# Seven products of quarters in place of eight in the second product of a feed forward, and low halves of weights made by adding transfers

## The chip, the cores and the metric

One core of a Trainium2 chip runs the whole program. The metric is its device time in microseconds (us), taken over several executions of the same compiled kernel. TensorE (PE) multiplies matrices, VectorE (DVE), ScalarE (ACT) and GpSimd (POOL) work element by element, and SyncE (SP) mainly issues transfers (DMA) between the large memory (HBM) and the on-chip memory (SBUF). Results of PE land in PSUM.

## The reference

Two layers of a decoder on one sequence of 512 tokens with 1024 channels, in float32. A layer mixes the tokens in three ways (pooling means, a state-space layer called S5, sparse attention), merges these, and then applies a squared-ReLU feed forward of width 4096. Cut to the part in question, with `x` 512 x 1024:

```python
def feed_forward_part(x):            # once in each of two layers
    h = jnp.square(jax.nn.relu(x @ w_ff1))        # 512 x 4096
    return layer_norm(ALPHA * x + h @ w_ff2, ln2_g, ln2_b)
```

The second product is `h @ w_ff2`, 512 x 4096 by 4096 x 1024. The next layer's S5 needs operands that depend on its parameters alone.

## The kernel before, in words

**One float32 product as three.** Every operand is split into a high half `hi` (the value rounded to the type that PE multiplies in one pass) and a low half `lo = value - hi`. `mm3_` (L91) issues three matmuls for each pair of blocks: hi by hi (L98), hi by lo and lo by hi (L99, L100). A matmul here is of 128 x 128 by 128 x 512.

**A weight.** `wload` (L69) loads 128 x 1024 weights (512 KB) by a transfer of SP into `wst` (two buffers), ACT casts it to `wh` (L82), and DVE, or in some stages POOL, subtracts to get `wl` (L85). `wh` and `wl` have four buffers each in the pool `wp`.

**The feed forward** (`ffn`, L1093, and `feed_forward`, L1224) runs in eight chunks c of 512 hidden channels. `up(c)` makes the chunk's hidden activations in four tiles m: 24 matmuls into PSUM `mm`, relu on ACT (L1102), square on DVE (L1103), split by ACT (L61) and DVE (L62). `down(c)` multiplies them by the chunk's four tiles of `w_ff2`: for each half of the output channels and each block `tb` of 128 tokens, `part` issues 12 matmuls into PSUM `s` or `t`, and DVE adds the result to `xm` (L1120). These are eight groups of 12, 96 matmuls, for a chunk's down, and 96 for its up. The program order is up(c+1), then down(c).

**What goes on beside it.** At the start of a feed forward POOL applies the affine part of the norm before it (`ln_affine`, L217: L222 and L223, 16 operations). In layer 0, `s5_ahead` (L533) then lets POOL build layer 1's S5 operands in four blocks r beside chunks 1 to 6: each loads `bc` (L501, SP), computes into one of two tiles `zwe` (L461 to L464, L514, L524 and others), and stores 1664 KB to `s5d` by SP. Weights `w0` for layer 1's first product are loaded during chunk 2; the weights of chunk 7 as its down begins.

**What sets the order.** A scheduler that simulates the engines' times fixes the order of the instructions of each engine when the program is built; loads of weights have high priority. An engine then runs its list strictly in that order, and each instruction waits for the semaphores that it names.

Of the kernel before, what the change touches and what calls it, by code (L numbers as in the profile page):

```python
# [18 lines left out]
DEPTH = 2  # L19
# [7 lines left out]
class Kern:  # L27
# [463 lines left out]
    def s5_operands(self, pool, i, r, zwe, eng, alone=False):  # L491
# [43 lines left out]
    def s5_ahead(self, i, after):  # L535

        with self.tc.tile_pool(name=f"s5a{i}", bufs=1, reuse_waits="tile") as pool:
            qs = [self.t(pool, [128, 3328], F32, f"zwe{k}") for k in range(2)]
            for r in range(5):
                with self.tc.issue_after(after):  # L540
                    if r < 2:
                        self.nc.gpsimd.memset(qs[r][:, 0:2304], 0.0)
                    if r < 4:
                        self.s5_operands(pool, i, r, qs[r % 2], self.nc.gpsimd, True)
# [548 lines left out]
    def ffn(self, i, xs, p0):  # L1093

        nc, v = self.nc, self.nc.vector

        def up(c):
            hs = []
            for m in range(4):
                ps = p0[m] if c == 0 else self.xw([self.wload(self.A["wf1"][i, 4 * c + m])])[0]  # L1100
                h = self.t(self.mt, [128, 512], F32, "mt")
                nc.scalar.activation(h, ps, AF.Relu)  # L1102
                v.tensor_tensor(h, h, h, OP.mult)  # L1103
                hh, hl = self.pair("ab"[c % 2])
                self.hi_lo(hh, hl, h)
                hs.append((hh, hl))
            return hs
# [22 lines left out]
        def down(c, hs, post):  # L1130
            W = self.A["wf2"]
            if c < 7:
                for half in range(2):
                    ws = [None] * 4
                    for kp in range(2):
                        ws[2 * half + kp] = self.wload(W[i, c, half, kp])
                    for tb in range(4):
                        part(hs, ws, tb, half, c)
# [84 lines left out]

    def feed_forward(self, i, xs, p0, w0p, g, b):  # L1224
        nc, A = self.nc, self.A
        up, down = self.ffn(i, xs, p0)
        how = ("aa", "aa", "am", "vv")

        def post(tb):
# [11 lines left out]
        for c in range(8):  # L1241
            nx = up(c + 1) if c < 7 else None
            if c == 1 and i < DEPTH - 1:
                ahead = self.s5_ahead(i + 1, self.affine.ins)
            if 1 <= c < 7 and i < DEPTH - 1:
                next(ahead, None)
            if c == 2 and i < DEPTH - 1:
                w0 = [self.wload(A["win"][i + 1, j], w0p, nc.vector) for j in range(4)]
            if c == 7 and i < DEPTH - 1:
                g, b = [], []  # L1250
                for q, tag, row in ((g, "hi_a", 4 + 4 * i), (b, "lo_a", 5 + 4 * i)):
# [107 lines left out]
```

## Time and profile before

| | us |
|---|---|
| median of 3 runs | 1770.89 |
| lowest and highest | 1769.59, 1772.9 |
| profiled execution | 1768.97 |
| its span, from first to last instruction | 1767.2 |
| PE busy in the span | 1672.5 (95%) |
| DVE, ACT, POOL busy | 1135.8 (64%), 711.8 (40%), 546.2 (31%) |

The profile shows one execution. Busy shares are means over stages with different limits, so a stage is read from windows and timelines of that stage. In a timeline a row gives start, duration, engine, line and operation, with out<-in, and in brackets the idle time before it with what ended it. The granted clock of PE is given as a share of 2.4 GHz: 1.00 is 2.4 GHz, 0.50 is 1.2 GHz.

### The profile page before, as it was taken

The numbers are of one execution on the slowest core, as the hardware profiler recorded it, in microseconds if no ns is written. First come the engines' busy times: TensorE is split into PE (matmuls) and PEld (weight loads), VectorE is DVE, ScalarE is ACT, GpSimd is POOL, SyncE is SP. The second block draws the span as 40 slices with busy tenths as digits, with TensorE's granted clock in tenths as the row PEclk, the third lists the DMA queues.
The fourth block names the chain that finished last, engine by engine and source line by source line (L and its number), as shares of the span: only waits on it lengthen the run. The fifth ranks groups of instructions, "written<-read, shape, count | busy, mean of one in ns | idle before, by whom it ended". The sixth has DMA issues, their size and how long they took to land.

```text
span 1767.2 us, 22544 instructions
## 1 busy us (share of the span) xinstructions
PE 1672.5 (95%) x8356; PEld 1397.7 (79%) x8356; DVE 1135.8 (64%) x2171; ACT 711.8 (40%) x1245; POOL 546.2 (31%) x636
## 2 busy tenths in 40 slices
PE   3969999999999999999998999999999999999996
PEld 2857887887779888888897788878787888888885
DVE  8797568676578656444576565867657774444447
ACT  2444336666534323233242442555564433222221
POOL 4993421322113999400033233122202050000002
PEclk9989999999999999999998999999999999999998
DMA  5313251111251246443316424211124133333331
GB/s 193 117 37 98 87 184 60 57 51 60 87 188 36 93 143 190 138 139 97 113 61 205 164 88 150 87 60 60 56 88 161 43 119 96 96 97 100 101 97 59
DMA packets 64334, 183.69 MB, mean 104 GB/s; under 512 B 12256, under 2 KB 21216, under 8 KB 63200
## 3 DMA queue, kind: packets, MB, share of 16 engines
q1 hardware_dynamic: 61632, 176.88, 30.9%
q10 hardware_dynamic: 2592, 5.38, 1.0%
q8 instruction: 65, 1.06, 0.3%
q14 instruction: 45, 0.37, 0.1%
HBM read 164.93 MB, written 17.30 MB: 103 GB/s over the span
## 4 chain that ended last, share of the span: by engine, by line
PE 78%; DVE 12%; POOL 4%; DMA 3%; ACT 2%; issue 1%; SPq 0%; DVEq 0%; ACTq 0%; POOLq 0%
PE mm L98 16%; PE mm L99 16%; PE mm L100 16%; PE s L99 4%; PE s L100 4%; PE s L98 4%; PE t L99 3%; PE t L100 3%; PE t L98 3%; PE o L834 3%; PE t L929 2%; DVE wl L85 1%; PE s L901 1%; PE s L900 1%; PE o L801 1%
## 5 line engine op out<-in xcount | busy, mean ns | idle before, releaser
L82 ACT CAST wh<-wst 128x1024 fp32r<-128x1024 f32 (+1 forms) x260 | 270.4, 1042 | 545.7 <-PE s L100 210.9
L85 DVE TENSOR_TENSOR wl<-wst,wh 128x1024 fp32r<-128x1024 f32 (+2 forms) x212 | 281.0, 1327 | 253.0 <-ACT wh L82 252.6
L98 PE MATMUL mm<-xh,wh 128*128 128x512 f32 (+1 forms) x1088 | 429.8, 395 | 6.6 <-ACT wh L82 5.4
L100 PE MATMUL mm<-xh,wl 128*128 128x512 f32 (+1 forms) x1088 | 420.2, 386 | 7.5 <-DVE wl L85 7.5
L99 PE MATMUL mm<-xl,wh 128*128 128x512 f32 (+1 forms) x1088 | 419.1, 385 | 0.0
L100 PEld LDWEIGHTS mm<-xh,wl 128*128 128x128 f32 x1088 | 205.5, 189 | 50.1 <-DVE wl L85 8.8
L98 PEld LDWEIGHTS mm<-xh,wh 128*128 128x128 f32 x1088 | 205.8, 189 | 44.9 <-ACT wh L82 5.9
L99 PEld LDWEIGHTS mm<-xl,wh 128*128 128x128 f32 x1088 | 206.0, 189 | 33.8
L85 POOL TENSOR_TENSOR wl<-wst,wh 128x1024 fp32r<-128x1024 f32 x48 | 122.2, 2546 | 239.2 <-ACT wh L82 233.5
L193 POOL TENSOR_TENSOR xm<-xm,ln_g 128x512 f32<-128x512 f32 x9 | 12.2, 1367 | 321.2 <-ACT xm L192 321.2
L906 ACT ACTIVATE P<-P,mx 128x512 f32<-128x512 f32 (+3 forms) x128 | 71.3, 559 | 63.5 <-DVE mx L904 63.0
L904 DVE CUSTOM_DVE_ANT_0 P<-s,mask 128x512 f32<-128x512 f32 (+3 forms) x128 | 59.6, 484 | 45.3 <-PE s L901 38.1
L62 DVE TENSOR_TENSOR Pl<-t,Ph 128x384 fp32r<-128x384 f32 (+1 forms) x96 | 57.3, 597 | 35.8 <-ACT Ph L61 35.5
L1120 DVE TENSOR_TENSOR xm<-xm,t 128x512 f32<-128x512 f32 x56 | 38.4, 686 | 54.1 <-PE t L100 51.2
L222 POOL TENSOR_TENSOR xm<-xm,hi_a 128x512 f32<-128x512 f32 x8 | 12.7, 1585 | 180.5 <-PE t L238 180.5
L222 POOL TENSOR_TENSOR xm<-xm,ln_g 128x512 f32<-128x512 f32 x16 | 30.2, 1886 | 121.6 <-PE t L238 121.6
L1120 DVE TENSOR_TENSOR xm<-xm,s 128x512 f32<-128x512 f32 x56 | 38.2, 682 | 41.6 <-PE s L100 41.6
L913 POOL TENSOR_SCALAR P<-P,sm,gate 128x128 f32<-128x128 f32 x32 | 15.3, 479 | 156.2 <-DVE sm L908 156.2
L61 ACT CAST Ph<-t 128x384 fp32r<-128x384 f32 (+1 forms) x96 | 48.1, 505 | 26.2 <-PE t L929 26.1
L98 PE MATMUL mm<-hi_a,wh 128*128 128x512 f32 x132 | 54.7, 414 | 2.1 <-DVE lo_a L318 2.1
L1103 DVE TENSOR_TENSOR mt<-mt 128x512 f32<-128x512 f32 x64 | 55.6, 869 | 0.0
L929 PE MATMUL t<-ident,P 128*128 128x128 f32 x320 | 51.8, 276 | 2.7 <-DVE P L913 2.7
(406 smaller groups left out, 3834.3 us busy)
## 6 DMA issues: line engine op xcount, KB each, us to landing
wst<-in_wf_dram SPq DMA_DIRECT2D x128, 512.0 KB, 3.5
wst<-in_win_dram SPq DMA_DIRECT2D x80, 512.0 KB, 3.3
wst<-in_wup_dram SPq DMA_DIRECT2D x24, 512.0 KB, 3.5
wst<-in_wout_dram SPq DMA_DIRECT2D x16, 512.0 KB, 4.2
s5d<-zwe SPq DMA_DIRECT2D x4, 1664.0 KB, 9.2
zwe<-s5d SPq DMA_DIRECT2D x4, 1664.0 KB, 9.1
xd<-xm SPq DMA_DIRECT2D x8, 512.0 KB, 4.9
w<-in_w_dram SPq DMA_DIRECT2D x8, 512.0 KB, 7.6
```

Source lines behind the costliest of these rows:

```text
L62: b = self.nc.vector.tensor_tensor(lo, src, hi.bitcast(F32), OP.subtract)
L82: self.nc.scalar.copy(wh, st)
L85: e.tensor_tensor(wl, st, wh.bitcast(F32), OP.subtract)
L98: mm(out, ah, bh, start=first and i == 0, stop=False, **kw)
L99: mm(out, ah, bl, start=False, stop=False, **kw)
L100: mm(out, al, bh, start=False, stop=last and i == n - 1, **kw)
L834: mm = lambda o, a, b, **k: nc.tensor.matmul(o, a, b, skip_group_check=True, **k)
L904: v.tensor_tensor_reduce(out=p, in0=ss[qb], in1=self.mask[:, 384 - 128 * qb:512], scale=-1.0, scalar=3e38, op0=OP.add, op1=OP.min, accum_o ...
L906: nc.scalar.activation(p, p, AF.Exp, bias=mx[:, qb:qb + 1], scale=-1.0, accum_out=c)
L929: nc.tensor.transpose(pt[:, n:n + 128], P[:, c:c + 128], self.ident)
L1103: v.tensor_tensor(h, h, h, OP.mult)
L1120: v.tensor_tensor(r, r, ps, OP.add)
```

## The change

Chunks 0 to 6 of the second product go by the Strassen-Winograd scheme. The product of a chunk (512 tokens x 512 hidden by 512 hidden x 1024) is cut into quarters: a11 to a22 of the activations (256 tokens by 256 hidden), b11 to b22 of the weights (256 hidden by 512 outputs). Four sums of activation quarters (`e1` to `e4`) and four of weight quarters (`t1` to `t4`) give seven products of 12 matmuls where eight were. The activations of a chunk lie in `big`, the pool of the first weights, are squared by ACT (`Square`), and seven combinations are split (`hi_lo`). The weights lie in `big` as well, and seven combinations of them are split by ACT and DVE into `wp`. The products go to PSUM tiles `s`, `t` and `o`; DVE adds them to `xm`, 14 times in a chunk; one sum that three quarters share is collected over the seven chunks in `AU` and added to `xm` at the end.

Apart from that: `wload(..., sums=True)`, for tiles m = 1 to 3 of every up, chunk 7's weights and layer 1's `w0`, makes `wl` in another way: ACT writes the negated weight, rounded to the type of `wl`, which is the negated high half, and a transfer issued by POOL adds the weight from HBM to it. The loads of `bc` and the stores to `s5d` are issued by POOL. The operands' blocks begin in chunks 1 to 4, `w0` loads at chunk 7, and chunk 7's weights during chunk 6. The order of the affine operations is rs3, rs2, rs0, rs1.

```diff
-    def wload(self, ap, pool=None, split=None):
+    def wload(self, ap, pool=None, split=None, sums=False):
...
             self.nc.scalar.copy(wh, st)
+            if sums:
+                self.nc.scalar.activation(wl, st, AF.Copy, scale=-1.0)
+                self.nc.gpsimd.dma_start(wl, ap, accum_op=OP.add)
+                return wh, wl
...
-            for r in (rs[3], rs[0], rs[1], rs[2]):
+            for r in (rs[3], rs[2], rs[0], rs[1]):
...
-        nc.sync.dma_start(bc, self.A["s5bc"][i, :, :, r * 64:(r + 1) * 64])
+        (gl if alone else nc.sync).dma_start(bc, self.A["s5bc"][i, :, :, r * 64:(r + 1) * 64])
...
-            for r in range(5):
+            for r in range(4):
...
-                if r:
-                    with self.tc.issue_after(self.loaded):
-                        self.nc.sync.dma_start(self.s5d[r - 1], qs[(r - 1) % 2])
+                    self.nc.gpsimd.dma_start(self.s5d[r], qs[r % 2])
...
+        def hidden(c, m, h):
+            ps = p0[m] if c == 0 else self.xw([self.wload(self.A["wf1"][i, 4 * c + m], sums=m > 0)])[0]
+            nc.scalar.activation(h, ps, AF.Relu)
+            nc.scalar.activation(h, h, AF.Square)
...
+            for k in range(2):
+                q = by2(self.t(big, [128, 1024], R, "wl", 4).bitcast(F32))
+                for m in range(2):
+                    hidden(c, 2 * k + m, q[:, m])
+                hs.append(q)
...
+            p11, p12, p22 = (split(q, self.pair("ab"[c % 2])) for q in (a11, a12, a22))
+            v.tensor_tensor(a22, a22, a21, OP.subtract)
+            e1 = esplit(a22, 1)
+            v.tensor_tensor(a21, a11, a21, OP.subtract)
+            v.tensor_tensor(a11, a11, a22, OP.add)
+            v.tensor_tensor(a12, a11, a12, OP.subtract)
+            e4 = esplit(a12, 4)
+            e3 = esplit(a21, 3)
+            e2 = esplit(a11, 2)
...
+            def split(x):
+                wh, wl = (self.t(self.wp, [128, 1024], R, q, 4) for q in ("wh", "wl"))
+                nc.scalar.copy(wh, x)
+                v.tensor_tensor(wl, x, wh.bitcast(F32), OP.subtract)
...
+                b11, b12, b21, b22 = load(0, 0), load(1, 0), load(0, 1), load(1, 1)
+                w11 = split(b11)
+                add(b11, b12)
+                t1 = split(b11)
+                w21 = split(b21)
+                w22 = split(b22)
+                add(b12, b22)
+                t3 = split(b12)
+                add(b11, b22)
+                t2 = split(b11)
+                add(b11, b21)
+                t4 = split(b11)
...
+            mul(p11, w11, A)
+            if c == 0:
+                for j in range(2):
+                    v.tensor_copy(AU[j], A[j])
+            else:
+                acc(u, A, plus)
+            mul(e1, t1, C)
+            acc(lambda j: r(3, j), C, minus)
+            mul(p12, w21, A, False)
+            acc(lambda j: r(0, j), A, plus)
+            mul(e4, w22, C, False)
+            acc(lambda j: r(1, j), C, minus)
...
+            mul(e3, t3, D)
+            acc(lambda j: r(3, j), D, minus)
+            mul(e2, t2, B)
+            acc(u, B, minus)
+            mul(p22, t4, D, False)
+            acc(lambda j: r(2, j), D, plus)
...
-            if 1 <= c < 7 and i < DEPTH - 1:
+            if 1 <= c < 5 and i < DEPTH - 1:
                 next(ahead, None)
-            if c == 2 and i < DEPTH - 1:
-                w0 = [self.wload(A["win"][i + 1, j], w0p, nc.vector) for j in range(4)]
+            if c == 7 and i < DEPTH - 1:
+                w0 = [self.wload(A["win"][i + 1, j], w0p, sums=True) for j in range(4)]
...
+            if c == 6:
+                self.w7 = [self.wload(A["wf2"][i, 7, half, kp], w7, sums=True) for half in range(2) for kp in range(2)]
```

`mul` issues for each of two blocks of 128 tokens six matmuls: two blocks of hidden channels by three parts. `acc` adds the two PSUM tiles on DVE (128 x 512 each).

The order shows what moves. First POOL, between the first and the second block of the operands in layer 0 (`ct`, `et`, `Zc`, `Wc` and `zwe` are tiles of that computation, `bc` its loaded input). Before:

```order
L461 TENSOR_TENSOR ct_1228_6400<-bc_6396,s_kre_127 128x8x16
L462 TENSOR_TENSOR ct_1229_6401<-bc_6396,s_kim_128 128x8x16
L461 TENSOR_TENSOR et_1175_6101<-zwe_1146_6011,s_pr_229 128x512
L462 TENSOR_TENSOR et_1176_6102<-zwe_1146_6011,s_pi_230 128x512
L514 COPY Wc_6399<-bc_6396 128x8x16
L463 TENSOR_TENSOR Zc_6398<-ct_1228_6400,ct_1229_6401 128x4x16
L464 TENSOR_TENSOR Zc_6398<-ct_1228_6400,ct_1229_6401 128x4x16
L463 TENSOR_TENSOR zwe_1146_6011<-et_1175_6101,et_1176_6102 128x4x64
L464 TENSOR_TENSOR zwe_1146_6011<-et_1175_6101,et_1176_6102 128x4x64
```

After (`wl_5939`, `wl_5974` and `wl_6008` are the low halves of tiles m = 1, 2, 3 of up(2)):

```order
L465 TENSOR_TENSOR ct_1258_6491<-bc_6487,s_kre_127 128x8x16
L466 TENSOR_TENSOR ct_1259_6492<-bc_6487,s_kim_128 128x8x16
L85 DMA wl_5939<-in_wf_dram 128x1024
L467 TENSOR_TENSOR zwe_1166_6074<-et_1195_6164,et_1196_6165 128x4x64
L468 TENSOR_TENSOR zwe_1166_6074<-et_1195_6164,et_1196_6165 128x4x64
L85 DMA wl_5974<-in_wf_dram 128x1024
L518 COPY Wc_6490<-bc_6487 128x8x16
L467 TENSOR_TENSOR Zc_6489<-ct_1258_6491,ct_1259_6492 128x4x16
L468 TENSOR_TENSOR Zc_6489<-ct_1258_6491,ct_1259_6492 128x4x16
L85 DMA wl_6008<-in_wf_dram 128x1024
L548 DMA s5d_97<-zwe_1166_6074 128x3328
```

Three adding transfers and the store of a finished block now stand between the operations of POOL, and each waits in line behind the operations ahead of it.

Then PE, where down(0) ends and up(2) goes on. Before, the last group of products (`s_5842`) is followed by the first tile of up(2), `mm_5862`, in the order of the program:

```order
L100 MATMUL s_5842<-wh_5796,lo_a_5558 128x512
L98 MATMUL s_5842<-wh_5796,hi_a_5564 128x512
L99 MATMUL s_5842<-wl_5797,hi_a_5564 128x512
L100 MATMUL s_5842<-wh_5796,lo_a_5565 128x512
L98 MATMUL mm_5862<-xh_1018_5032,wh_5858 128x512
L99 MATMUL mm_5862<-xl_1019_5033,wh_5858 128x512
L100 MATMUL mm_5862<-xh_1018_5032,wl_5859 128x512
```

After, PE has put matmuls that need no low half ahead (`mm_5978` and `mm_6012` are tiles m = 2 and 3 of up(2), `s_6211` and `s_6212` the first product of down(1)):

```order
L102 MATMUL mm_5978<-xh_1018_5032,wh_5973 128x512
L103 MATMUL mm_5978<-xl_1019_5033,wh_5973 128x512
L102 MATMUL s_6211<-wh_6179,hi_b_5724 128x512
L102 MATMUL s_6212<-wh_6179,hi_b_5724 128x512
L102 MATMUL mm_6012<-xh_1018_5032,wh_6007 128x512
L103 MATMUL mm_6012<-xl_1019_5033,wh_6007 128x512
L103 MATMUL s_6211<-wl_6180,hi_b_5724 128x512
```

Ten rows on, the first matmul that reads the first low half made by an adding transfer, `wl_5939`:

```order
L104 MATMUL s_6212<-wh_6179,lo_b_5725 128x512
L102 MATMUL s_6212<-wh_6179,hi_b_5724 128x512
L103 MATMUL s_6212<-wl_6180,hi_b_5724 128x512
L104 MATMUL s_6212<-wh_6179,lo_b_5725 128x512
L104 MATMUL mm_5943<-xh_1018_5032,wl_5939 128x512
```

Sixteen matmuls of later work stand ahead of the 22 of `mm_5943` that begin with the reading of `wl_5939`.

## Rows read from the trace of the kernel before

**Rows 1.** The page: span, and busy time (share of the span) and instructions of each engine.

```profile
span 1767.2 us, 22544 instructions
...
PE 1672.5 (95%) x8356; PEld 1397.7 (79%) x8356; DVE 1135.8 (64%) x2171; ACT 711.8 (40%) x1245; POOL 546.2 (31%) x636
```

**Rows 2.** Windows of one chunk in layer 0 and in layer 1: us, busy by engine, clock, DMA.

```profile
593.00:637.00 44.00, 44.00 (x196) 36.44 (x195) 22.73 (x26) 12.69 (x16) 43.17 (x87) 1.00 0.34 110
1490.00:1534.00 44.00, 44.00 (x196) 36.44 (x195) 20.09 (x24) 13.37 (x17) 0.00 (x0) 1.00 0.32 96
```

**Rows 3.** Timeline of PE: start, us, line, operation; up(1) and down(0) of layer 0.

```profile
571.39 0.40 PE L98 MATMUL mm<-xh,wh 128*128 128x512 f32 x1
...
593.18 0.39 PE L98 MATMUL t<-wh,hi_a 128*128 128x512 f32 x1
```

**Rows 4.** Timeline of DVE in a chunk of layer 0 after POOL's work.

```profile
740.26 0.69 DVE L1120 TENSOR_TENSOR xm<-xm,s 128x512 f32<-128x512 f32 x1 [2.03 <-PE s L100]
...
742.98 0.69 DVE L1120 TENSOR_TENSOR xm<-xm,t 128x512 f32<-128x512 f32 x1 [2.03 <-PE t L100]
...
752.00 1.23 DVE L85 TENSOR_TENSOR wl<-wst,wh 128x1024 fp32r<-128x1024 f32 x1 [3.57 <-ACT wh L82]
...
753.14 0.68 DVE L1103 TENSOR_TENSOR mt<-mt 128x512 f32<-128x512 f32 x1
...
754.51 0.69 DVE L62 TENSOR_TENSOR lo_b<-mt,hi_b 128x512 fp32r<-128x512 f32 x1 [0.69 <-ACT hi_b L61]
```

**Rows 5.** ACT's lines over the span: count | busy us, mean ns | idle before, releasers.

```profile
L82 ACT CAST wh<-wst 128x1024 fp32r<-128x1024 f32 (+1 forms) x260 | 270.4, 1042 | 545.7 <-PE s L100 210.9 <-PE mm L99 199.0 <-DMA wst<-in_win_dram 58.7
...
L1102 ACT ACTIVATE mt<-mm 128x512 f32<-128x512 f32 x58 | 34.2, 590 | 0.0
...
L61 ACT CAST hi_a<-mt 128x512 fp32r<-128x512 f32 x32 | 19.9, 622 | 62.7 <-DVE mt L1103 62.7
...
L647 ACT ACTIVATE st<-st 128x512 f32<-128x512 f32 x8 | 5.1, 635 | 33.5 <-DMA st<-across 33.5
```

**Rows 6.** Timeline of POOL in layer 0: affine of the norm, then operands of layer 1.

```profile
556.38 1.29 POOL L222 TENSOR_TENSOR xm<-xm,ln_g 128x512 f32<-128x512 f32 x1 [61.41 <-PE t L238]
...
562.40 2.27 POOL L222 TENSOR_TENSOR xm<-xm,ln_g 128x512 f32<-128x512 f32 x1
...
585.05 2.03 POOL L542 MEMSET zwe<- 128x2304 f32 x1
...
589.76 0.84 POOL L462 TENSOR_TENSOR ct<-bc,s_kim 128x128 f32<-128x128 f32 x1
...
619.22 0.40 POOL L462 TENSOR_TENSOR ct<-bc,s_kim 128x128 f32<-128x128 f32 x1
...
729.48 0.74 POOL L464 TENSOR_TENSOR zwe<-et,et 128x256 f32<-128x256 f32 x1
```

**Rows 7.** Timeline of DVE beside POOL's affine operations.

```profile
571.33 1.77 DVE L1103 TENSOR_TENSOR mt<-mt 128x512 f32<-128x512 f32 x1
...
573.03 2.31 DVE L85 TENSOR_TENSOR wl<-wst,wh 128x1024 fp32r<-128x1024 f32 x1
```

**Rows 8.** The page's DMA issues: out, in, queue, count, KB each, us to landing.

```profile
wst<-in_wf_dram SPq DMA_DIRECT2D x128, 512.0 KB, 3.5
...
s5d<-zwe SPq DMA_DIRECT2D x4, 1664.0 KB, 9.2
```

**Rows 9.** SP's issues on line 501: duration in ns, min/median/max.

```profile
L501 SPq DMA_DIRECT2D bc<-in_s5bc_dram x8: 540/551/653, 8.0 to 621.9; - x8
```

**Rows 10.** Window of POOL's operand building in layer 0: us, POOL busy (x), clock, DMA.

```profile
585.05:730.30 145.25, 141.47 (x254) 1.00 0.45 142
```

**Rows 11.** PE's wait for a reload, and the window behind it.

```profile
PE t L589 <- DMA zwe<-s5d: 5.8, 1, 5.8
...
936.00:942.00 6.00, 3.46 (x16) 2.88 (x17) 1.55 (x4) 1.69 (x3) 2.23 (x2) 0.50 1.00 376
```

More of the change, by code (lines that the diff above doesn't have):

```diff
@@ L1091, in out_proj, with ffn @@
         return rs, p0
-    def ffn(self, i, xs, p0):
+    def ffn(self, i, xs, p0, big, fp):
         nc, v = self.nc, self.nc.vector
+        by2 = lambda q: q.rearrange("p (k t) -> p k t", k=2)
+        AU = [self.t(fp, [128, 512], F32, f"au{j}") for j in range(2)]
+        def hidden(c, m, h):
+            ps = p0[m] if c == 0 else self.xw([self.wload(self.A["wf1"][i, 4 * c + m], sums=m > 0)])[0]
+            nc.scalar.activation(h, ps, AF.Relu)
+            nc.scalar.activation(h, h, AF.Square)
@@ L1097, in up @@
         def up(c):
             hs = []
[L1099 to L1107, printed above, removed]
+            if c == 7:
+                for m in range(4):
+                    h = self.t(self.mt, [128, 512], F32, "mt")
+                    hidden(c, m, h)
+                    hh, hl = self.pair("ab"[c % 2])
+                    self.hi_lo(hh, hl, h)
+                    hs.append((hh, hl))
+                return hs
@@ new lines, in up, with split @@
+            for k in range(2):
[3 more added lines that the diff above has]
+                hs.append(q)
+            f = slice(0, 256), slice(256, 512)
+            a11, a12, a21, a22 = hs[0][:, :, f[0]], hs[1][:, :, f[0]], hs[0][:, :, f[1]], hs[1][:, :, f[1]]
+            def split(src, pair):
+                hh, hl = (by2(q) for q in pair)
+                self.hi_lo(hh, hl, src)
+                return hh, hl
@@ new lines, in esplit @@
+            def esplit(src, n):
+                return split(src, [self.t(fp, [128, 512], R, f"e{n}{x}") for x in "hl"])
+            p11, p12, p22 = (split(q, self.pair("ab"[c % 2])) for q in (a11, a12, a22))
[5 more added lines that the diff above has]
+            e4 = esplit(a12, 4)
@@ new lines, in up, with products, load, mul @@
+            e3 = esplit(a21, 3)
+            e2 = esplit(a11, 2)
+            return p11, p12, p22, e1, e2, e3, e4
+        def products(c, hs):
+            p11, p12, p22, e1, e2, e3, e4 = hs
+            W = self.A["wf2"]
+            def load(half, kp):
+                x = self.t(big, [128, 1024], R, "wh", 4).bitcast(F32)
+                self.loaded = nc.sync.dma_start(x, W[i, c, half, kp]).ins
+                return x
+            def split(x):
+                wh, wl = (self.t(self.wp, [128, 1024], R, q, 4) for q in ("wh", "wl"))
+                nc.scalar.copy(wh, x)
+                v.tensor_tensor(wl, x, wh.bitcast(F32), OP.subtract)
+                return wh, wl
+            add = lambda a, b: v.tensor_tensor(a, a, b, OP.add)
+            with self.tc.high_priority():
+                b11, b12, b21, b22 = load(0, 0), load(1, 0), load(0, 1), load(1, 1)
[10 more added lines that the diff above has]
+                t4 = split(b11)
+            r = lambda n, j: xs[2 * (n // 2) + j][:, (n % 2) * 512:(n % 2 + 1) * 512]
+            def mul(a, w, ps, first=True):
+                for j in range(2):
+                    s = slice(j * 128, (j + 1) * 128)
+                    terms = [((a[0][:, k, s], a[1][:, k, s]), (w[0][:, k * 512:(k + 1) * 512], w[1][:, k * 512:(k + 1) * 512])) for k in range(2)]
+                    self.mm3(ps[j], terms, first=first, skip=True)
+            def acc(dst, ps, op):
+                for j in range(2):
+                    with self.tc.high_priority():
+                        v.tensor_tensor(dst(j), dst(j), ps[j], op)
+            u, minus, plus = lambda j: AU[j], OP.subtract, OP.add
+            A, C = [self.psum("s") for j in range(2)], [self.psum("t") for j in range(2)]
+            mul(p11, w11, A)
+            if c == 0:
+                for j in range(2):
+                    v.tensor_copy(AU[j], A[j])
[7 more added lines that the diff above has]
+            acc(lambda j: r(1, j), C, minus)
+            D, B = [self.psum("o"), self.psum("s")], [self.psum("s"), self.psum("t")]
+            mul(e3, t3, D)
[5 more added lines that the diff above has]
+            if c == 6:
+                for j in range(2):
+                    for n, op in ((1, minus), (2, plus), (3, minus)):
+                        v.tensor_tensor(r(n, j), r(n, j), AU[j], op)
@@ L1132, in down @@
             if c < 7:
[L1133 to L1138, printed above, removed]
+                products(c, hs)
             else:
-                ws = [self.wload(W[i, c, half, kp]) for half in range(2) for kp in range(2)]
+                ws = self.w7
                 return blocks(hs, ws, post)
@@ L1225, in feed_forward, with feed @@
         nc, A = self.nc, self.A
-        up, down = self.ffn(i, xs, p0)
+        with ExitStack() as stack:
+            fp = stack.enter_context(self.tc.tile_pool(name=f"ff{i}", bufs=1, reuse_waits="tile"))
+            self.feed(i, xs, p0, w0p, g, b, fp, stack)
+    def feed(self, i, xs, p0, w0p, g, b, fp, stack):
+        nc, A = self.nc, self.A
+        up, down = self.ffn(i, xs, p0, w0p, fp)
         how = ("aa", "aa", "am", "vv")
@@ L1256, in feed_forward @@
             hs = nx
+            if c == 5 and i == DEPTH - 1:
+                w7 = w0p
+            elif c == 5:
+                next(ahead, None)
+                w7 = stack.enter_context(self.tc.tile_pool(name=f"w7{i}", bufs=1, reuse_waits="tile"))
+            if c == 6:
+                self.w7 = [self.wload(A["wf2"][i, 7, half, kp], w7, sums=True) for half in range(2) for kp in range(2)]
         if i < DEPTH - 1:
```

3 lines of the change are left out of this document (1 added, 2 removed).

## The prediction

> **What bounds the kernel now.** I read the page first: TensorE (PE) is busy 1672.5 of the span's 1767.2 us [rows 1], so only a stretch in which PE is not full could hide a saving of matmuls. Next, the windows of one chunk of either feed forward: in 44 us PE is busy for all 44, at a granted clock of 1.00. DVE is busy 22.73 and 20.09 of them, ACT 12.69 and 13.37; POOL is busy 43.17 in layer 0 and not at all in layer 1 [rows 2]. So PE sets the time of both feed forwards, and POOL is full, unnoticed, in the first. The timeline of PE gives the length of a chunk: up(1) starts at 571.39 and down(0) at 593.18, so the 96 matmuls of an up take 21.79 us, 5.45 per tile of 24, and a chunk of two such halves 43.6 [rows 3]. Whatever an edit puts on the other engines is free until it makes PE wait.
>
> **What it removes.** Seven products of 12 matmuls replace eight: 84 for 96 in a chunk, in chunks 0 to 6 of two layers, 12 x 7 x 2 = 168 matmuls of 128x512. Two accumulations that follow each other at PE's pace start at 740.26 and 742.98 with 12 matmuls between them, 2.72 us [rows 4]. So PE loses 168 / 12 x 2.72 = 38.1 us, 19.05 in each layer, and a chunk shrinks to 43.6 - 2.72 = 40.9. Nothing else of PE's work changes; the end follows this term unless PE waits for something new.
>
> **What it adds beside PE.** DVE: before, a chunk holds eight splits of weights (1.23), four squarings (0.68), four splits of activations and eight accumulations (0.69) [rows 4]: 9.84 + 2.72 + 8.28 = 20.8, which the window of layer 1 confirms (20.09). After, it holds one split for the up, seven for the products and four additions of weights (12 x 1.23), four quarter sums (0.68), seven splits of activations and fourteen accumulations (21 x 0.69): 14.76 + 2.72 + 14.49 = 32.0 of 40.9, 78%. ACT: eleven casts (1.04), three negated copies (0.635 for half the width, so 1.04 taken from the cast of the same width), four relu and four squares (0.59) and seven casts (0.62) [rows 5]: 14.6 + 4.7 + 4.3 = 23.6 us, 58%. Both fit under PE on the average of a chunk. I cost them at nothing there; the cover is gone where they start late or run slower.
>
> **The start of each feed forward.** There the cover is thin: the first chunk must make seven weight splits, four sums and seven activation splits before PE has used up up(1). In layer 0 POOL runs its 16 affine operations from 556.38 on [rows 6], and beside these the same DVE operations take 1.77 instead of 0.68 and 2.31 instead of 1.23 [rows 7]. Cost: nothing at best (up(1)'s 21.8 us cover it), at worst the 11 us by which 32.0 of work at an average slowdown of about a third passes one chunk. I take 3.5 for each layer, a third, since up(1) hides most of it.
>
> **The adding transfers.** Three of an up's four low halves are now a negated copy on ACT and a transfer that adds the weights, issued by POOL. The trace of before shows neither an issue by POOL nor an adding transfer, so two sizes are unknown. X, issue to landing: the plain load of the same 512 KB lands in 3.5 us and 1664 KB in 9.2 [rows 8], so 5.7 us for 1152 KB, 2.5 us of moving for 512 KB; if reading the target costs the moving twice, 6.0. Bounds 3.5 and 8 (two plain landings and an issue), taken 5. d, what one issue takes of POOL: SP's plain issue takes 0.55 [rows 9] and POOL's own operations of 512 columns 1.29 to 2.27 [rows 6]; bounds 0.55 and 2.3, taken 0.55, the only row that is an issue.
>
> The Trainium skill, "DMA: Bandwidth & Descriptors", section "Anatomy of one DMA — SWDGE (gpsimd) path", puts such a transfer from POOL at about 2.0 us and bytes over 436 GB/s, 3.2 us as an estimate here; by that alone X would lie under my lower bound and the sum 1.8 us lower. Against it stands "Collectives: The Full Stack", section "The bandwidth ceiling: the fold count and why AG ≠ RS ≠ AR": an add pushes twice the reads. No run here shows either.
>
> What X costs the buffers decide: four pairs serve the seven products and the four tiles. The pair of tile m=1 comes free behind the fifth product; 48 matmuls (two products and tile m=0, 10.9 us) lie from there to m=1's first use, of which ACT's cast and negated copy take 2.1 and the issue 0.55. So X up to 8.2 costs nothing if transfers overlap; one by one, three must land in the 19 us from there to m=3's first use, so up to some 6.2 each.
>
> **POOL's queue in layer 0.** POOL builds the next layer's state-space operands beside chunks 1 to 6, 254 operations from 585.05 to 730.2 [rows 6, 10], its loads (formerly on SP) and its stores of 1664 KB now also issued by POOL, and the adding transfers stand between these operations. The first late one, for up(2), stands where before the operation at 619.22 stood [rows 6], and its place in POOL's order stands with the change. Six issues are now ahead of it (three adding, three loads): 6d = 3.3. POOL's operations are also stretched by DVE's two-input work: one form, `ct<-bc,s_kim`, takes 0.84 and 0.40 us [rows 6]; with each form at its shortest, the 254 take 38 us less than their 145.25 [rows 10]. DVE's operations that read two tiles of SBUF fill 15.2 of 43.6 (35%) before and 22.2 of 40.9 (54%) after, so the 38 grow by 55% to 59: some 5 us for each of the four blocks, which take (145.25 - 2 x 2.03) / 4 = 35.3 now. POOL therefore comes to the transfer at 619.2 + 3.3 + 4.9 = 627.4 and it lands at 627.4 + 0.55 + 5 = 633.0. PE needs it at 571.4 + 21.8 + 19.05 + 3.5 (start) + 5.45 (m=0) + 3.6 (some 16 other matmuls put ahead) = 624.8. Stall 8.2 us, that is 7d + X - 0.7. A later block takes 35.3 + 5 + 5d = 43.05 (three adding transfers, a store and a load) against PE's 40.9: 2.15 x 3 = 6.5 more. The stores of 9.2 us in the same queue delay the transfers behind them by up to 4 each; I take 2 in all. After a wait PE also runs slowly: where it waited 5.8 us for zwe, the granted clock was 0.50 in the 6 us behind [rows 11], the 1.2 GHz level, and PE's 3.46 busy us there cost 1.7 more than at full clock: taken 2. Layer 0: 3.5 + 8.2 + 6.5 + 2 + 2 = 22.2.
>
> **Layer 1.** POOL has nothing else to do there. Start 3.5; chunk 7's four weight loads now wait for the big buffers of the products, 2; slips of m=1's landing 1.5: 7.
>
> **Sum.** -38.1 + 22.2 + 7 = -8.9: 1768.97 becomes 1760.1. The profiled execution lies 1.9 below the median of the runs (1770.89), so in their terms 1762.0. What is late next is the first adding transfer of each chunk in layer 0, with POOL as what it waits for.
>
> **Rivals.**
> A. Nothing waits but the starts: -38.1 + 7 = -31, 1740. For it: PE full, DVE at 78%, and the operands needed only in the next layer. Against it: POOL at 43.17 of 44.
> B. Slower: POOL's queue paces layer 0. One mechanism, d: an issue as long as POOL's shortest operation of 512 columns, 1.29, and X = 6. First stall 7 x 1.29 + 6 - 0.7 = 14.3; blocks 5 x 1.29 - 0.6 = 5.85, x 3 = 17.6; queue 4, clock 6, start 3.5: 45.4, and 8 in layer 1. -38.1 + 53.4 = +15.3, 1786. Layer 0's loss grows by 7 + 15 = 22 us for each us of d, so it decides from d = 0.55 + 8.9 / 22 = 0.95.
> C. The adding transfers themselves are too slow: X = 8 one by one. Three take 24 us where 18.6 are to be had, so each of 14 chunks loses 5.4: 76, and layer 0's 22 on top: +60, 1831. Against it: 512 KB in 3.5, the DMA share at 0.32 to 0.34 [rows 2].
> D. No change: stalls eat the gain, d between 0.8 and 1.1: 1771, 3.5 either way.
> The Trainium skill, "DMA: Bandwidth & Descriptors", section "Latency and other measured facts", gives the first byte of a POOL issue as about 1 us, which it lays to POOL's own work of writing the descriptors; an estimate of d = 1 from it would be case D, 1770. No row of POOL bears it out yet.
>
> **How the numbers follow.** Forecast .42 (its own range, -20 to -2 us: 1751 to 1769); A .18, B .20, C .07, D .13. The range of 8 in 10 leaves out C and the tails of A and B: 1736 to 1790. Changes under 0.2% (3.5 us) can't be told from none here. Faster: A .18, .36 of the forecast's .42 and .02 of D: .56. Within: .06 of the forecast and .10 of D: .16. Slower: B, C and .01 of D: .28.
>
> **What the changed profile would show.** The matmul term: 84 matmuls between two ups and PE full in layer 1, chunk near 40.9; wrong if PE idles there in each chunk. The transfers: landing near 5; over 8 speaks for C. The queue: PE idle in layer 0 waiting for an adding transfer to the low half, near 625 by before's time, some 8 us, with the granted clock at 0.50 behind it; POOL's issues of 0.55, and over 0.95 speaks for B; POOL's operands ending near 763 instead of 730. The forecast is wrong at its root if PE's waits in layer 0 name DVE or ACT instead, or if there are none.

## The result and the profile after

The changed kernel takes 1790.3 us (median of 4 runs, 1789.0 to 1798.1) against 1771.4 for the kernel before: a ratio of 1.0116, 95% interval 1.0085 to 1.0147. It is 1.2% slower, and 28 us above the forecast. The page of the profile after, with the lines that answer to [rows 1, 8] (in the lines of DMA: out, in, queue, count, KB, us to landing):

```profile
span 1789.4 us, 22738 instructions
...
PE 1650.7 (92%) x8188; PEld 1367.3 (76%) x8188; DVE 1253.5 (70%) x2345; ACT 862.4 (48%) x1447; POOL 602.5 (34%) x698
...
wl<-in_wf_dram POOLq DMA_DIRECT2D x50, 512.0 KB, 7.9
...
s5d<-zwe POOLq DMA_DIRECT2D x4, 1664.0 KB, 9.9
```

PE runs 168 matmuls less, as counted, but its busy time falls by 21.8 us only, not 38.1, and it idles 139 us instead of 95. So 16 us went into matmuls that kept it busy longer and 44 into waits. The adding transfers land in 7.9 us (the median of 50), where I had taken 5.

To place the loss, read the transposes of the normed activations that stand before and after each feed forward, and PE's last matmul, in PE's timeline. Before:

```profile
555.64 1.04 PE L238 MATMUL t<-ident,xm 128*128 128x128 f32 x8
...
892.39 1.03 PE L238 MATMUL t<-ident,xm 128*128 128x128 f32 x8
...
1408.79 1.03 PE L238 MATMUL t<-ident,xm 128*128 128x128 f32 x8
...
1750.75 0.39 PE L100 MATMUL mm<-wh,lo_b 128*128 128x512 f32 x1
```

After:

```profile
556.15 1.04 PE L242 MATMUL t<-ident,xm 128*128 128x128 f32 x8
...
919.00 1.03 PE L242 MATMUL t<-ident,xm 128*128 128x128 f32 x8
...
1436.72 1.04 PE L242 MATMUL t<-ident,xm 128*128 128x128 f32 x8
...
1774.96 0.39 PE L104 MATMUL mm<-wh,lo_b 128*128 128x512 f32 x1
```

Layer 0's feed forward takes 362.85 us instead of 336.75, layer 1's 338.24 instead of 341.96. Each should have become 19.05 shorter, so layer 0 loses 45.1 and layer 1 15.3 against that; between them 1.3 are added. I call these two numbers the losses, and every experiment below is read by them. Each is taken from one profiled execution; the times of one kernel's executions spread by 1 us (plain transfers), 9 us (the change) and up to 17 us (two adding transfers per up), so a difference of a few us between two losses shows little.

Windows of the changed kernel, each from one chunk's product with `e2` to the next (columns as in [rows 2]: busy time and count of PE, its weight loads, DVE, ACT and POOL, then granted clock and DMA): four of layer 0 (the first from the start of down(0)), one of layer 1.

```profile
593.70:609.60 15.90, 14.35 (x62) 10.95 (x60) 15.87 (x19) 6.05 (x9) 15.74 (x27) 1.00 0.23 75
609.60:666.50 56.90, 46.42 (x180) 35.80 (x181) 33.61 (x38) 23.39 (x30) 53.13 (x93) 0.88 0.46 134
666.50:711.10 44.60, 41.60 (x182) 33.57 (x181) 35.69 (x38) 23.21 (x31) 44.05 (x73) 1.00 0.58 175
711.10:759.20 48.10, 42.60 (x182) 34.81 (x181) 33.76 (x37) 21.22 (x29) 45.97 (x67) 0.96 0.51 150
...
1487.90:1530.70 42.80, 41.16 (x182) 33.59 (x180) 29.60 (x39) 22.92 (x30) 2.60 (x3) 1.00 0.52 135
```

Without waits a chunk takes 40.8. The first late chunk takes 56.9: PE is idle 10.5 us, and its 180 matmuls, 40.8 at full clock, take 46.4; the granted clock is 0.88 over the window. No chunk is free of loss, in layer 1 either. The first row shows DVE and POOL both full at the start. What PE waits for in the late chunk, in the timelines of ACT, POOL and PE in layer 0:

```profile
614.03 1.06 ACT L84 ACTIVATE wl<-wst 128x1024 fp32r<-128x1024 f32 x1
```

```profile
632.71 0.94 POOL L85 DMA_DIRECT2D wl<-in_wf_dram  x1
633.39 1.04 POOL L467 TENSOR_TENSOR zwe<-et,et 128x256 f32<-128x256 f32 x1
...
635.06 0.88 POOL L85 DMA_DIRECT2D wl<-in_wf_dram  x1
635.66 0.58 POOL L518 COPY Wc<-bc 128x128 f32<-128x128 f32 x1
```

```profile
624.95 0.73 PE L102 MATMUL s<-wh,hi_b 128*128 128x512 f32 x2 [1.77 <-ACT wh L1156]
...
638.55 0.80 PE L104 MATMUL mm<-xh,wl 128*128 128x512 f32 x1 [8.38 <-DMA wl<-in_wf_dram]
```

The negated copy is done at 615.1, POOL issues the transfer 17.6 us later, when it has come to it in its line, it lands at 638.5, and PE stands for 8.4 us. Ahead of that PE had already stood for 1.8 us for a cast of ACT, and its clock had fallen to 0.50 behind that wait, and was 0.50 again behind the longer one (windows of PE: busy, clock, DMA):

```profile
625.83:629.24 3.41, 3.41 (x9) 0.50 0.35 132
638.55:642.89 4.34, 4.34 (x10) 0.50 1.07 213
```

Half of these 7.75 us, 3.9, is what the clock cost here as an estimate: 1.7 behind the short wait and 2.2 behind the long one. The rest of the 5.6 us I can't place: PE is busy for more than 40.8 in the next window too, at a clock of 1.00.

In layer 1 POOL is idle, and PE still waits for the same tile:

```profile
PE mm L104 <- DMA wl<-in_wf_dram: 10.6, 10, 2.6
```

(total us, times, longest; window 1420 to 1780). And the records of POOL's issues, the answer to [rows 9]:

```profile
L85 POOL DMA_DIRECT2D wl<-in_wf_dram x50 | 45.8, 915 | 381.1 <-DVE wl L1137 244.1 <-ACT wl L84 99.3 <-PE mm L103 19.6
...
L548 POOL DMA_DIRECT2D s5d<-zwe x4 | 3.5, 866 | 0.4 <-POOL zwe L468 0.4
```

A record lasts 0.92 us, not 0.55. But POOL starts its next operation 0.68 us (633.39 after 632.71) or 0.60 us (635.66 after 635.06) behind the start of an issue, before the record has ended. What an adding transfer takes of POOL's line is thus some 0.6 us, not 0.92.

### The profile page after: what moved, and what is told of

Same layout as the page of the kernel before. It is cut to its first block, busy times and chain, and to the rows that moved or that the text cites. A ratio compares the mean times of both kernels' runs of the same rounds, so it can differ in the third digit from the quotient of the medians.

```text
span 1789.4 us, 22738 instructions
## 1 busy us (share of the span) xinstructions
PE 1650.7 (92%) x8188; PEld 1367.3 (76%) x8188; DVE 1253.5 (70%) x2345; ACT 862.4 (48%) x1447; POOL 602.5 (34%) x698
## 4 chain that ended last, share of the span: by engine, by line
PE 58%; DVE 15%; DMA 8%; POOL 7%; issue 7%; ACT 4%; SPq 0%; POOLq 0%; DVEq 0%; ACTq 0%
PE mm L104 13%; PE mm L102 13%; PE mm L103 12%; DMA wl<-in_wf_dram 4%; PE o L835 3%; PE s L103 2%; PE t L930 2%; PE s L104 2%; PE s L102 2%; DMA wst<-in_wf_dram 2%; DMA wst<-in_win_dram 1%; DVE wl L89 1%; ACT wh L82 1%; PE s L902 1%; PE s L901 1%
## 5 line engine op out<-in xcount | busy, mean ns | idle before, releaser
L104 PE MATMUL mm<-xh,wl 128*128 128x512 f32 (+1 forms) x1088 | 425.4, 391 | 41.8 <-DMA wl<-in_wf_dram 34.9
L82 ACT CAST wh<-wst 128x1024 fp32r<-128x1024 f32 (+2 forms) x204 | 211.0, 1037 | 302.1 <-PE mm L103 106.1
L104 PEld LDWEIGHTS mm<-xh,wl 128*128 128x128 f32 x1088 | 206.9, 190 | 93.2 <-DMA wl<-in_wf_dram 43.1
L1157 DVE TENSOR_TENSOR wl<-wh,wh 128x1024 fp32r<-128x1024 f32 x98 | 122.9, 1256 | 168.2 <-ACT wh L1156 168.2
L89 DVE TENSOR_TENSOR wl<-wst,wh 128x1024 fp32r<-128x1024 f32 (+3 forms) x102 | 135.2, 1327 | 71.0 <-ACT wh L82 70.8
L1156 ACT CAST wh<-wh 128x1024 fp32r<-128x1024 f32 x98 | 102.8, 1049 | 169.9 <-PE mm L103 96.8
L85 POOL DMA_DIRECT2D wl<-in_wf_dram x50 | 45.8, 915 | 381.1 <-DVE wl L1137 244.1
L905 DVE CUSTOM_DVE_ANT_0 P<-s,mask 128x512 f32<-128x512 f32 (+3 forms) x128 | 59.7, 485 | 49.5 <-PE s L902 42.1
L1160 DVE TENSOR_TENSOR wh<-wh,wh 128x1024 f32<-128x1024 f32 x56 | 70.0, 1250 | 1.2
L226 POOL TENSOR_TENSOR xm<-xm,ln_g 128x512 f32<-128x512 f32 x16 | 27.4, 1711 | 121.6 <-PE t L242 121.6
L84 ACT ACTIVATE wl<-wst 128x1024 fp32r<-128x1024 f32 x54 | 57.0, 1055 | 10.8 <-DMA wst<-in_win_dram 5.9
```

The costliest lines, as they stand in the source:

```text
L104: mm(out, al, bh, start=False, stop=last and i == n - 1, **kw)
L905: v.tensor_tensor_reduce(out=p, in0=ss[qb], in1=self.mask[:, 384 - 128 * qb:512], scale=-1.0, scalar=3e38, op0=OP.add, op1=OP.min, accum_o ...
L1156: nc.scalar.copy(wh, x)
L1157: v.tensor_tensor(wl, x, wh.bitcast(F32), OP.subtract)
L1160: add = lambda a, b: v.tensor_tensor(a, a, b, OP.add)
```

## The experiments

The table gives the losses of all kernels, in us, each from its own profile as above; "ratio" is against the kernel before, with its 95% interval.

| kernel | median | ratio | loss in layer 0 | in layer 1 |
|---|---|---|---|---|
| the change | 1790.3 | 1.0116 (1.0085 to 1.0147) | 45.1 | 15.3 |
| ups' low halves by DVE | 1746.9 | 0.9859 (0.9840 to 0.9877) | 14.4 | 0.0 |
| no operands on POOL | 1772.0 | 1.0008 (0.9995 to 1.0022) | 22.1 | 13.3 |
| POOL's other issues back on SP | 1797.4 | 1.0144 (1.0110 to 1.0178) | 45.9 | 12.3 |
| plain transfers | 1761.4 | 0.9938 (0.9923 to 0.9954) | 30.6 | 0.0 |
| two adding transfers per up | 1790.8 | 1.0096 (1.0061 to 1.0131) | 42.3 | 18.7 |
| more staging in layer 1 | 1783.7 | 1.0075 (1.0054 to 1.0096) | 42.9 | 6.8 |
| no adding transfer at all | 1741.1 | 0.9818 (0.9796 to 0.9840) | 7.9 | 0.0 |
| ups by DVE, no operands | 1735.6 (one run) | | 4.9 | 0.0 |
| adding transfers alone, eight products | 1779.7 | 1.0040 (1.0024 to 1.0056) | 8.6 longer than before | 0.0 longer |

**1. The ups' low halves by DVE.**

```diff
-            ps = p0[m] if c == 0 else self.xw([self.wload(self.A["wf1"][i, 4 * c + m], sums=m > 0)])[0]
+            ps = p0[m] if c == 0 else self.xw([self.wload(self.A["wf1"][i, 4 * c + m])])[0]
```

> The changed kernel with the low halves of tiles m = 1 to 3 of every up made by DVE's subtraction again; chunk 7's weights and layer 1's w0 keep their adding transfers. DVE then has 32.0 + 3 x 1.23 = 35.7 us of 40.9 per chunk (87%). Theory Q (the adding transfers stand in POOL's line and land late; they cost the 45.7 us that layer 0 loses and the 13.4 of layer 1): layer 0 loses 5 to 10 (its start, DVE stretched beside POOL), layer 1 up to 2, so -38 + 10 = 1743, between 1737 and 1755, and PE waits for no transfer to a low half in the ups. Rival D (DVE is what the transfers were to relieve, and becomes the bound): DVE full in layer 0, PE waits for the splits there, 1770 or more.

Measured 1746.9, 24 us faster than before and 43 faster than the change. The first window is a chunk of layer 0, the second one of layer 1:

```profile
610.50:652.60 42.10, 41.95 (x180) 33.57 (x181) 38.43 (x42) 19.78 (x27) 41.56 (x51) 1.00 0.43 143
...
1500.00:1540.80 40.80, 40.80 (x182) 33.80 (x181) 32.75 (x41) 19.83 (x27) 0.00 (x0) 1.00 0.32 104
```

In layer 1 PE is full, and the whole 19.05 us are there. DVE, busy 38.43 of 42.1 in layer 0, holds. Theory Q's time came, within its range; layer 0's loss of 14.4 is above the 5 to 10 that it had, and experiment 9 shows why. The three adding transfers per up, with ACT's negated copies for them, cost the 43 us, and they relieved an engine that did not bound.

**2. No building of operands on POOL.**

```diff
-                    self.s5_operands(pool, i, r, qs[r % 2], self.nc.gpsimd, True)
+                    self.nc.gpsimd.memset(qs[r % 2], 0.0)
```

> The changed kernel without the building of layer 1's S5 operands on POOL: its tiles are cleared (2 to 3 us each) and stored, its input loads are left out, so layer 1's S5 part is computed from zeros. Theory Q: POOL issues each adding transfer of layer 0 as soon as ACT has written the negated weights; layer 0's loss falls from 45.7 to that of layer 1 (13.4) and some 3 of its start, so 1790 - 30 = 1760, between 1752 and 1768. Rival T (the transfers are slow in themselves, POOL's line matters little): layer 0 keeps over 30 of its loss, 1775 or more.

Measured 1772.0, between the two theories. Layer 0's loss halves, from 45.1 to 22.1, so POOL's building is worth some 23 us; but layer 1 loses 13.3 still and layer 0 22.1, with POOL left with its affine operations and the clearing: something other than the line costs as much. PE's longest wait there, 5.2 us, is for a cast of ACT, which itself stood 2.8 us for a load into a staging buffer.

**3. Loads of `bc` and stores to `s5d` issued by SP again.**

```diff
-        (gl if alone else nc.sync).dma_start(bc, self.A["s5bc"][i, :, :, r * 64:(r + 1) * 64])
+        nc.sync.dma_start(bc, self.A["s5bc"][i, :, :, r * 64:(r + 1) * 64])
...
-                    self.nc.gpsimd.dma_start(self.s5d[r], qs[r % 2])
+                if r:
+                    with self.tc.issue_after(self.loaded):
+                        self.nc.sync.dma_start(self.s5d[r - 1], qs[(r - 1) % 2])
                 yield
+            with self.tc.issue_after(self.loaded):
+                self.nc.sync.dma_start(self.s5d[3], qs[1])
```

> The changed kernel with the loads of bc and the stores to s5d issued by SP again, as before the change; the adding transfers stay on POOL. Theory Q: POOL's line is shorter by three issues of 0.8 ahead of the first late adding transfer and by a load and a store (0.8 + 1.2) in each block, and no store of 1664 KB lies ahead of an adding transfer in its queue: 2.4 + 3 x 2 + 2 = 10 us less, 1780, between 1775 and 1786. Rival S (SP waits in its own line for POOL's blocks and the weight loads behind it come late): 1790 or slower, with PE waiting for a cast behind a load.

Measured 1797.4; layer 0's loss stays (45.9). POOL issues the first late transfer at 630.48 instead of 632.71, but SP now stands in its own line (SP's timeline):

```profile
615.69 2.12 SPq L79 DMA_DIRECT2D wst<-in_wf_dram  x2
631.72 0.55 SPq L505 DMA_DIRECT2D bc<-in_s5bc_dram  x1
632.38 1.47 SPq L79 DMA_DIRECT2D wst<-in_wf_dram  x2
```

The load of `bc` waits until 631.72 for POOL to give back its buffer, and the weights of two tiles wait behind it. That is the place that rival S named, and its time came, but not its sign: ACT casts these two tiles at 668.26 only, without waiting for their loads, and PE's long waits in layer 0 (12.8, 7.6 and 4.7 us) are for adding transfers, none for a cast (timelines of ACT and PE):

```profile
668.26 2.01 ACT L82 CAST wh<-wst 128x1024 fp32r<-128x1024 f32 x2
```

```profile
636.12 0.80 PE L104 MATMUL mm<-xh,wl 128*128 128x512 f32 x1 [12.77 <-DMA wl<-in_wf_dram]
...
688.86 0.79 PE L104 MATMUL mm<-xh,wl 128*128 128x512 f32 x1 [7.60 <-DMA wl<-in_wf_dram]
```

With the edit the scheduler also ordered PE and POOL anew: 52 matmuls instead of 66 stand between the first product with `e2` and the first late reading, and POOL comes to the first transfer of the next up at 678.95 instead of 673.71. So the saving that Q expected did not come, and why is not settled: this run does not price POOL's other issues by themselves.

**4. Adding transfers in the kernel before, with its eight products.** The edit is the `sums` branch of `wload` and `sums=m > 0` in the up, put into the kernel before.

> The kernel before (eight products, everything else as before) with one edit: the low halves of tiles m = 1 to 3 of every up by ACT's negated copy and an adding transfer of POOL. Theory Q: the transfers cost much in layer 0, where they stand among POOL's operations (10 to 25 us), and less in layer 1, where POOL is idle (0 to 6): 1771 + 10 to 30, taken 1790. Rival T (landing of 7.9 us is too late anywhere): both layers lose alike, 13 each, 1797. Rival N (they cost only where the products are seven): within 1768 to 1775.

Measured 1779.7: 9 us slower, all of it in layer 0 (8.6, with one wait of PE for such a transfer, 3.3 us); layer 1 takes the same 341.96. The transfers land in 8.2 us there too, so a landing of that length costs nothing by itself: T falls, and Q's place holds at half the size that I took, just under its range and above N's. What the chunk of seven products lacks beside this one is the question of the next experiments.

**5. Plain transfers in place of the adding ones.**

```diff
-                self.nc.gpsimd.dma_start(wl, ap, accum_op=OP.add)
+                self.nc.gpsimd.dma_start(wl, ap)
```

> The changed kernel with POOL's adding transfers made plain ones of the same size from the same address to the same tiles (the weights replace the negated copy, so the low halves hold other values); issues, waits and buffers stay as they are. Theory Q+X (landing of 7.6 to 8.1 us, longer than the 5 I took because the add reads the target too, is what the chunks of layer 1 wait for): a plain transfer lands in some 4 to 5.5 us, layer 1's loss falls from 15.3 to under 5, layer 0's by about as much: 1790 - 20 = 1770, between 1764 and 1776. Rival P (what POOL issues is slow whatever it does, or the loads beside it are): it lands in 7 or more, and the time stays within 1784 to 1794.

```profile
wl<-in_wf_dram POOLq DMA_DIRECT2D x50, 512.0 KB, 5.1
```

Measured 1761.4, some 3 us below the range. The same bytes land in 5.1 us, layer 1's loss is gone (0.0), layer 0's falls by 14.5. The record of an issue falls too, from 0.92 to 0.55 us, but POOL's next operation beside the operands starts 0.56 to 0.65 us behind it, as with adding (0.58 to 0.68), so POOL's line is no shorter. Without the 2.8 us that the adding takes, layer 1 loses nothing. Layer 0 keeps 30.6: two waits for transfers in POOL's line, 15.5 us together, and what follows from them.

**6. Two adding transfers per up.**

```diff
-            ps = p0[m] if c == 0 else self.xw([self.wload(self.A["wf1"][i, 4 * c + m], sums=m > 0)])[0]
+            ps = p0[m] if c == 0 else self.xw([self.wload(self.A["wf1"][i, 4 * c + m], sums=m > 1)])[0]
```

> The changed kernel with adding transfers for the tiles m = 2 and 3 of the ups alone; m = 1 gets its low half by DVE. Theory S (slack: m = 1's pair of buffers comes free only 10.9 us before its use, m = 2's 13.6 and m = 3's 16.4, while cast, copy, issue and landing take some 11): layer 1's chunks fall from 42.5 to 43.7 to 41.2 or less, its loss to under 5, and layer 0's first wait shrinks by the 5.45 us that m = 2 is needed later; 1790 - 11 - 10 = 1769, between 1760 and 1776. Rival N (each adding transfer costs alike, by what it takes from the DMA engines or from POOL): two thirds of the 43 us that all three cost stay, 1776 or more.

Measured 1790.8 (runs from 1779.4 to 1796.8): layer 1 loses 18.7, no less than with three, and PE's first long wait in layer 0 is 10.1 us, where S had expected it shorter. Theory S falls. N's bound is met, but not its two thirds: two cost as much as three, within the spread of the runs. The timelines of DVE and ACT in layer 1, and SP's, show what is late:

```profile
1488.30 1.21 DVE L89 TENSOR_TENSOR wl<-wst,wh 128x1024 fp32r<-128x1024 f32 x1
1491.24 1.22 DVE L89 TENSOR_TENSOR wl<-wst,wh 128x1024 fp32r<-128x1024 f32 x1
```

```profile
1489.54 8.82 SPq L79 DMA_DIRECT2D wst<-in_wf_dram  x4
```

```profile
1493.76 1.05 ACT L82 CAST wh<-wst 128x1024 fp32r<-128x1024 f32 x1 [4.72 <-DMA wst<-in_wf_dram]
1494.72 1.05 ACT L84 ACTIVATE wl<-wst 128x1024 fp32r<-128x1024 f32 x1
```

There are two staging buffers. The load of m = 2 is issued at 1489.54, when DVE's split of m = 0 is done with one; ACT waits 4.7 us for it, and only then come copy, issue (1496.17) and landing. A chain from the staging buffer, through a DVE that is behind with accumulations (m = 0 was cast by 1485.7, and DVE, busy without a gap, comes to its split at 1488.30), not the wait for a pair `wh`, `wl`, sets when this transfer starts. That m = 1's split lengthens the chain here is likely, but not shown.

**7. Two more staging buffers in layer 1.**

```diff
-    def wload(self, ap, pool=None, split=None, sums=False):
+    def wload(self, ap, pool=None, split=None, sums=False, stage=None):
...
-            st = self.t(self.wp, [128, n], F32, "wst", 2)
+            st = self.t(stage or self.wp, [128, n], F32, "wst", 2)
...
-            ps = p0[m] if c == 0 else self.xw([self.wload(self.A["wf1"][i, 4 * c + m], sums=m > 0)])[0]
+            ps = p0[m] if c == 0 else self.xw([self.wload(self.A["wf1"][i, 4 * c + m], sums=m > 0, stage=fp if i and m else None)])[0]
```

> The changed kernel with two more staging buffers wst in layer 1, for the loads of tiles m = 1 to 3 of the ups; nothing else. My theory S on the slack of the pairs wh and wl fell (with two adding transfers layer 1 lost 18.7 us, more than with three). Theory W: the load of a tile waits for a staging buffer that the split of m = 0 on DVE, or the copy of the tile before on ACT, gives back late; load (4 to 6), cast and copy (2.1), issue (0.9) and landing (7.6) follow one after the other from there. With the buffers layer 1's chunks fall from 42.5 to 45.3 to at most 41.3, its loss from 15.3 to under 4, and the time to 1778, between 1774 and 1783. Rival B (the landing beside other loads is too long whatever the buffers): chunks stay above 42, 1786 or more.

Measured 1783.7, just above W's range. Layer 1's loss falls from 15.3 to 6.8 by the buffers alone: W is right on the place. Not under 4: POOL now issues two transfers back to back, and the landings are longer, 8.8 us at the median where the change has 7.7 in the same window (POOL's timeline, and the landing in 1480 to 1720, min/median/max):

```profile
1493.32 1.83 POOL L85 DMA_DIRECT2D wl<-in_wf_dram  x2 [26.81 <-DVE wl L1137]
```

```profile
DMA to landing us min/median/max: 5.4/8.8/12.2
```

So part of its rival B may hold as well; how the rest divides I did not try.

**8. No adding transfer at all.** As 1, and `w0` and chunk 7's weights are split by DVE.

```diff
-                w0 = [self.wload(A["win"][i + 1, j], w0p, sums=True) for j in range(4)]
+                w0 = [self.wload(A["win"][i + 1, j], w0p, nc.vector) for j in range(4)]
...
-                self.w7 = [self.wload(A["wf2"][i, 7, half, kp], w7, sums=True) for half in range(2) for kp in range(2)]
+                self.w7 = [self.wload(A["wf2"][i, 7, half, kp], w7, nc.vector) for half in range(2) for kp in range(2)]
```

> The changed kernel with no adding transfer at all: as in the kernel where DVE makes the ups' low halves (1747), and DVE also subtracts for chunk 7's weights and layer 1's w0. If those eight transfers cost something too (PE waited 3.4 us at the end of layer 0's feed forward), 1741 to 1746; if they relieve DVE there, 1748 to 1753. Taken 1745.

Measured 1741.1, so those eight transfers cost something too: 1.8% faster than before and the fastest complete kernel here. The wait of 3.4 us that PE has in experiment 1's kernel at the end of layer 0's feed forward is gone.

**9. Ups by DVE, and no operands on POOL.** The edits of 1 and 2 together.

> The ups' low halves by DVE, and POOL's building of layer 1's S5 operands left out (tiles cleared and stored; layer 1's S5 part is computed from zeros). Theory C (the 1.1 to 2.3 us by which layer 0's chunks exceed 40.8 come from DVE's and POOL's operations stretching each other): layer 0's chunks fall to 40.8 to 41.0 as in layer 1, and the time to 1747 - 8 = 1739. Rival L (they come from something else in layer 0, such as the loads of the weights): chunks stay at 42, 1745 or more.

Measured 1735.6 in one run; a chunk of layer 0:

```profile
652.50:693.30 40.80, 40.80 (x182) 33.78 (x181) 32.81 (x41) 19.84 (x26) 0.00 (x0) 1.00 0.33 104
```

Every chunk of layer 0 before the last takes 40.8, as in layer 1, where with the operands they take 41.9 to 43.1. That excess of experiment 1 is thus the price of POOL's building beside DVE's work: DVE's 42 operations of a chunk took 38.43 us there, its 41 take 32.81 here. Of L nothing is left, as far as one run can tell.

## Why the prediction was wrong

The measured terms, in place of those of the sum: layer 0 lost 45.1, not 22.2, and layer 1 15.3, not 7. In layer 0 that is 2.3 at the start, 16.1 in the first late chunk and 26.7 in the five chunks behind it (3.8, 7.3, 7.6, 3.4 and 4.6), where the sum had 3.5, 10.2 (stall and clock) and 8.5 (blocks and stores). The later chunks are the largest miss.

**The step that failed: the slack of X.** "So X up to 8.2 costs nothing if transfers overlap" counted from the pair `wh`, `wl` and left out the staging buffers. X came to lie under 8.2, at 7.9, and layer 1 lost 15.3 us instead of 7, with ten waits of PE for these transfers, 10.6 us together. Experiment 7 gives 8.5 of these back with buffers, experiment 5 all with a shorter landing. The same step failed in layer 0: three of the five later chunks (7.6, 3.4 and 4.6) lie behind the end of POOL's building, so it can't hold them up, and experiment 2 leaves a loss of 22.1 there without any building. In the last of the three some 3 us have another cause, since experiment 9, without these transfers, has them as well.

**The adding transfer's size, X: mis-sized.** I took 5, between bounds of 3.5 and 8; it is 7.9. The 6.0 that I had worked out for an add that moves its target too was nearer, and was short as well. The plain transfer lands in 5.1. The Trainium skill's estimate for a plain one ("DMA: Bandwidth & Descriptors", "Anatomy of one DMA — SWDGE (gpsimd) path", 3.2) is exceeded by these runs, which have other transfers beside it; its account of a ReduceScatter, whose add reads two sources ("Collectives: The Full Stack", "The bandwidth ceiling: the fold count and why AG ≠ RS ≠ AR"), points the way that 5.1 against 7.9 goes.

**POOL's line in layer 0: the right kind, the first wait right by luck.** PE stood 8.4 us where 8.2 were forecast, but both ends came over 5 us later than forecast. POOL reached the transfer at 632.7, not 627.4: the same operations were stretched by some 8.7 us, not the 4.9 I took, and two operations of 512 columns (2.0 us) that stood behind the place before now stand ahead of it, which I overlooked; the three loads took 2.4 (0.8 each) of the 3.3 for issues, since the three adding transfers were issued during the affine operations. DVE was busy 15.87 of 15.90 us in the first part of that stretch. PE reached the reading at 630.2, not 624.8, behind its wait of 1.8 for ACT and a stretch at the lower clock. And this transfer landed in 5.8 us, not in the median's 7.9. PE's clock behind that wait cost 2.2 us, as an estimate, where I took 2; another 1.7 came ahead of it, behind the wait for ACT, for which the sum had nothing. The later blocks, from store to store 40.5, 46.4 and 34.2 us, took 121.1 together, against 129.2 forecast: POOL's line did not grow as the sum has it. An issue's size d was nearly right: 0.6 us of POOL's line for an adding transfer or a store and 0.8 for a load of `bc`, against 0.55, although its record lasts 0.92.

**The matmul term was right.** 38.1 us were forecast; experiments 1, 5, 8 and 9 each show 19.0 of them in layer 1, and chunks of 40.80 (forecast 40.9).

**DVE and ACT beside PE: right for the change.** 32.0 and 23.6 us a chunk were forecast; a chunk of layer 1 shows 29.6 and 22.9, and PE's waits in the feed forwards name neither for more than 2 us at a time. Three splits more on DVE fit in layer 1 (experiment 1); in layer 0 DVE then passes PE's pace beside POOL's building, by 1.1 to 2.3 us a chunk.

**The start: near in layer 0, wrong in layer 1.** I took 3.5 for each. From the transposes to the first product with `e2`, layer 0 takes 53.4 us, 2.3 more than layer 1's 51.1, where nothing is lost. The 11 us that I gave as the worst were DVE's added time; 32.0 and a third are 42.7, which pass a chunk of 40.9 by 1.8 only.

**The rivals.** B had nearly the price, a loss of 45.4 in layer 0 and 1786 in all, but by coincidence: its condition, d over 0.95 us, did not hold, its first stall of 14.3 was 8.4, and its blocks, each longer by 5.85 than a chunk, were on the mean no longer (40.4). C named the landing, and X came near its 8, but with a serial limit that these runs do not show. A and D fail with the time, 1740 and 1771. I had put X near the plain landing and the slack at its best, although PE had no slack in any chunk.

**What stays open:** how layer 0's 45.1 divide by cause. Taking POOL's building away gives 23.0 back, but experiment 9 against 1 shows that with three splits more on DVE 9.5 of such a removal are DVE's relief and not the line; the plain transfer gives 14.5. The parts overlap and were not separated further.

## What to carry to other kernels

Before work is moved off an engine to save it, ask whether that engine ends any wait: here DVE did not end PE's long waits, and the transfers that relieved it put POOL's line, a landing and a staging buffer on the path of an engine that is full. A transfer whose issue stands in an engine's line between long work is as late as that work; a load for the busiest engine belongs in a line that holds nothing else. Count slack from the first buffer of the chain, the staging one, not from the last.

## What the runs showed of the hardware

- An adding transfer of 512 KB issued by POOL lands in 7.9 us, a plain one of the same bytes in 5.1, and SP's plain load in 3.5 before the change, beside fewer other transfers (a DMA share of 0.32 to 0.34 in a chunk, where the change has 0.46 to 0.58).
- The record of an adding transfer's issue lasts 0.92 us on POOL and a plain one's 0.55, but beside the operands POOL's next operation starts some 0.6 us behind either.
- POOL's building of operands took 145 us before and 173 after the change, there with 17 issues and some short waits among its operations. With it DVE's 42 operations of a chunk took 38.43 us (experiment 1), without it 41 took 32.81 (experiment 9).
- A wait costs PE more than itself: in the chunk that came late first the granted clock was 0.50 behind a wait of 1.8 us and again behind the one of 8.4, for 3.4 and 4.3 us of matmuls, which cost 1.7 and 2.2 us as an estimate.
